# An order among the uses of gathered rows on VectorE, in the expert layer of a two-block model

## The chip, the cores and the metric

The kernel runs on one core of a Trainium2 chip. The metric is device time in microseconds, the median of three runs. The engines are named by what they do: TensorE (PE: matmuls, and PEld: loads of the stationary operand), VectorE (DVE), ScalarE (ACT), GpSimd (POOL) and SyncE (SP), which issues most transfers.

## What is computed

One sequence of 512 tokens plus 16 meta tokens, model width 1024, goes through two blocks. The first mixes tokens (an mLSTM and an attention with a forget gate) and ends in a layer of 16384 experts of one neuron each, of which every token uses 128. The second is a feed-forward layer, a hybrid mixer and a second feed-forward layer. Only the expert layer matters here. Cut to that:

```
def _peer(x, w_query, sub_keys, u_emb, v_emb):      # x: 512 tokens x 1024
    qh = (xb @ w_query).reshape(tb, 8, 2, 128)
    scores = einsum('thpc,hpnc->thpn', qh, keys32)   # 8 heads, 2 halves, 128 keys
    val, idx = lax.top_k(scores, 16)
    ...
    top_s, pos = lax.top_k(cand, 16)
    ids = ...                                        # 128 expert numbers a token
    gate = softmax(top_s)
    act = gelu(einsum('ted,td->te', u_emb[ids], xb))
    return einsum('te,ted->td', gate * act, v_emb[ids])
```

`u_emb` and `v_emb` are 16384 x 1024 float32.

## The kernel before

The expert layer is the method `peer` (L610). It treats the 512 tokens in two ways at once.

The first 384 tokens are computed densely, over all experts, on TensorE. The 16384 experts are 128 blocks of 128. For a block, 24 matmuls give the hidden activations (tile `hp`, a product of the split tokens `xh`, `xl` with a block of u), ScalarE applies the gelu, VectorE multiplies with the gates (`weigh`, L983, the product at L989), ScalarE and VectorE split the result into a high part `eh` and a low part `el` (L245, L250), and 18 matmuls add the block's share of the output into the PSUM tiles `o` (`apply`, L995). Every weight tile is split likewise by `unit` (L144): SyncE loads it into `wr` (L149), ScalarE rounds it to `wh` (L151), and VectorE or GpSimd makes the rest `wl` (L152).

The last 128 tokens are done by rows. Each has 128 experts, so there are 128 slots. For slot n, GpSimd gathers one row of u for each of the 128 tokens by an indirect transfer (tile `row`, 128 x 1024 float32, L643), and VectorE multiplies it with the tokens and sums over the width into a column of `hd3` (L659, a custom instruction and a read of its accumulator). After 128 slots `hd3` holds all activations; ScalarE applies the gelu and VectorE the gates (L661, L662). Then 128 rows of v are gathered in the same way, and each is multiplied by its column of `hd3` and added onto `xtok` (L664 for the first, L666 for the others). The rows share six buffers (`AHEAD + 2`). `own` (L638) issues gather n, and the use of row n - 4; both are placed behind a given VectorE instruction (`behind`, L649), which is how the gathers are paced. 40 gathers are issued while the gates of the dense part are made; the other 216 are spread over the loop of the second half, each behind an L989 product (variable `ws[-1][2]`):

```
                    while len(got) < EARLY + (256 - EARLY) * max(0, spent - REST) // (total - REST):
                        own(ws[-1][2])
```

That loop goes over the 128 blocks in an order that mixes 64 blocks whose activations were made earlier and parked in DRAM (tile `hg`) with 64 that are made now (tile `hd`), so one pass of a pair is one `hd`, one `hg`, 24 + 36 matmuls, and three or four gathers and uses.

The Python code doesn't fix the order in which an engine takes its instructions. A scheduler orders each engine's instructions by their dependencies and its own estimate of times; on the chip an engine then takes them strictly in that order, and one that waits holds all behind it. Uses of v rows depend on one another through `xtok`. Uses of u rows do not: each writes its own column of `hd3`.

Of the kernel before, what the change touches and what calls it, by code (L numbers as in the profile page):

```python
# [94 lines left out]
class Kern:  # L95
# [514 lines left out]
    def peer(self, y):  # L610
        nc, tc, a = self.nc, self.tc, self.a
# [9 lines left out]
        with ExitStack() as ctx:  # L621
# [11 lines left out]
            hd3 = Z.tile([128, 128], F32, name="hd3")  # L633
            rows = {n: a[n].rearrange("a b d -> (a b) d") for n in ("u", "v")}
            got = []
            done = [0]

            def own(after):  # L638

                n = len(got)  # L640
                e, sl = ("u", "v")[n // 128], n % 128
                got.append(Z.tile([128, D], F32, name="row", bufs=AHEAD + 2))
                ld = gp.indirect_dma_start(out=got[n], out_offset=None, in_=rows[e],  # L643
                                           in_offset=bass.IndirectOffsetOnAxis(ap=ids[:, sl:sl + 1], axis=0))
                behind(ld, after)
                if n >= AHEAD:
                    use(after)

            def behind(x, after):  # L649
                tc.add_manual_dep(x.ins, after.ins.name, mybir.DependencyInfo(  # L650
                    mybir.DependencyClass.Sync, mybir.DependencyReason.DATA), reason="pace the gathers")

            def use(after):
                n = done[0]
                done[0] += 1
                e, sl = ("u", "v")[n // 128], n % 128
                row = got[n]
                if e == "u":
                    x = v.tensor_tensor_reduce(row, row, xtok, 1.0, 0.0, OP.mult, OP.add, hd3[:, sl:sl + 1])  # L659
                    if sl == 127:  # L660
                        s.activation(hd3, hd3, AF.Gelu)  # L661
                        v.tensor_tensor(hd3, hd3, gate3, op=OP.mult)  # L662
                elif sl == 0:
                    x = v.tensor_scalar(xtok, row, hd3[:, 0:1], None, op0=OP.mult)  # L664
                else:
                    x = v.scalar_tensor_tensor(xtok, row, hd3[:, sl:sl + 1], xtok, op0=OP.mult, op1=OP.add)  # L666
                behind(x, after)

            with ExitStack() as c1:
                pool1 = lambda n, b=1, **k: c1.enter_context(tc.tile_pool(name=n, bufs=b, reuse_waits="tile", **k))  # L670
# [285 lines left out]
            with ExitStack() as c2:  # L956
# [69 lines left out]
                while done[0] < 256:  # L1026
                    use(ws[-1][2])
# [894 lines left out]
```

## Time and profile before

| | |
|---|---|
| Median of 3 runs | 3293.35 us (3289.94 to 3294.42) |
| The profiled execution: its own time | 3301.91 us |
| its span on the core | 3300.1 us |
| TensorE matmul busy | 3172.1 us, 96% of the span |
| VectorE busy | 1862.5 us, 56% |
| ScalarE busy | 1183.1 us, 36% |
| GpSimd busy | 1064.4 us, 32% |
| Mean granted clock of TensorE | 0.962 |
| First and last use of a u row | 680.7 and 1356.4 us from the span's start |
| First and last use of a v row | 1359.5 and 1788.8 us |

Times within the span are microseconds from its start. A busy share is an average over stages with different limits, so a change to one stage is read in that stage's stretch of the span: the busy time and the granted clock (1.00 is 2.4 GHz, 0.5 is 1.2 GHz) in windows, the waits there, and the order in time of single instructions. In a row of waits, "A <- B" means that A was idle until B ended.

### The profile page before, as it was taken

How to read it: one execution, taken by the hardware profiler on the slowest of the kernel's cores; microseconds unless marked ns; L12 is line 12 of the kernel's file. 1: busy time of each engine (PE TensorE's matmuls, PEld its weight loads, DVE VectorE, ACT ScalarE, POOL GpSimd, SP SyncE). 2: the span in 40 equal slices, each digit the busy share in tenths (PEclk: the TensorE clock that was granted, in tenths of full speed). 3: DMA queues.
4: the chain of work that ended last, by engine and by line, in shares of the span. 5: the costliest groups of instructions: out<-in, count | busy, mean ns of one | idle time of the engine just before them, and what ended most of it. 6: DMA issues, size and time to landing. Idle time of an engine off the chain costs nothing. (4 is left out here: it accounts for less than half of the span.)

```text
span 3300.1 us, 46734 instructions
## 1 busy us (share of the span) xinstructions
PE 3172.1 (96%) x18396; PEld 2794.9 (85%) x18396; DVE 1862.5 (56%) x3481; ACT 1183.1 (36%) x1915; POOL 1064.4 (32%) x676
## 2 busy tenths in 40 slices
PE   8999999799999898999998999989999999989998
PEld 7776788799998787888887999989888889778887
DVE  4342568987755555777887433266434445564324
ACT  3242433344443232333333322235544422332222
POOL 1000134332246675778886211030211002231101
PEclk8888999899999899999999999989999989989999
DMA  3110233377788877889986332232221143423233
GB/s 115 46 48 26 76 97 100 125 265 282 283 301 303 293 272 273 298 317 322 335 307 203 96 91 87 89 118 73 86 68 62 64 136 112 141 77 95 92 93 101
DMA packets 201476, 525.29 MB, mean 159 GB/s; under 512 B 19044, under 2 KB 82440, under 8 KB 199720
## 3 DMA queue, kind: packets, MB, share of 16 engines
q1 hardware_dynamic: 149544, 341.53, 31.5%
q0 software_dynamic: 40624, 142.96, 12.4%
q10 hardware_dynamic: 11088, 37.82, 2.9%
q8 instruction: 144, 2.36, 0.3%
q14 instruction: 76, 0.62, 0.1%
HBM read 470.85 MB, written 51.38 MB: 158 GB/s over the span
## 5 line engine op out<-in xcount | busy, mean ns | idle before, releaser
L151 ACT ACTIVATE wh<-wr 128x1024 fp32r<-128x1024 f32 (+2 forms) x549 | 560.2, 1030 | 1139.7 <-PE fm L89 352.0
L152 DVE TENSOR_TENSOR wl<-wr,wh 128x1024 fp32r<-128x1024 f32 (+1 forms) x371 | 443.0, 1197 | 252.0 <-ACT wh L151 240.7
L152 POOL TENSOR_TENSOR wl<-wr,wh 128x1024 fp32r<-128x1024 f32 (+1 forms) x178 | 438.9, 2480 | 225.1 <-ACT wh L151 224.0
L89 PE MATMUL hp<-xh,wh 128*128 128x384 f32 (+1 forms) x1080 | 377.7, 350 | 0.0
L89 PE MATMUL hp<-xh,wl 128*128 128x384 f32 (+1 forms) x1080 | 373.0, 345 | 4.4 <-DVE wl L152 3.2
L89 PE MATMUL hp<-xl,wh 128*128 128x384 f32 (+1 forms) x1080 | 376.1, 348 | 0.0
L643 POOL DMA_INDIRECT row<-in_u_dram,ids x128 | 196.8, 1538 | 327.0 <-DVE oh L935 213.9
L89 PE MATMUL fm<-xl,wh 128*128 128x264 f32 (+2 forms) x1080 | 280.0, 322 | 0.0
L89 PE MATMUL fm<-xh,wh 128*128 128x264 f32 (+2 forms) x1080 | 277.3, 320 | 1.2 <-DVE u L1173 1.0
L89 PE MATMUL fm<-xh,wl 128*128 128x264 f32 (+2 forms) x1080 | 275.6, 318 | 0.0
L89 PE MATMUL o<-wl,eh 128*128 128x512 f32 x768 | 243.0, 398 | 22.3 <-DVE wl L152 21.9
L659 DVE CUSTOM_DVE_ANT_0 row<-row,xtok 128x1024 f32<-128x1024 f32 x128 | 168.1, 1319 | 164.6 <-DMA row<-in_u_dram,ids 162.8
L89 PE MATMUL mm<-xh,wh 128*128 128x264 f32 (+1 forms) x864 | 245.7, 342 | 14.1 <-ACT wh L151 10.6
L89 PE MATMUL o<-wh,eh 128*128 128x512 f32 x768 | 240.8, 395 | 9.0 <-ACT wh L151 9.0
L89 PE MATMUL mm<-xl,wh 128*128 128x264 f32 (+1 forms) x864 | 245.4, 341 | 1.1 <-DVE xl L252 1.1
L89 PE MATMUL o<-wh,el 128*128 128x512 f32 x768 | 240.5, 395 | 0.0
L89 PE MATMUL mm<-xh,wl 128*128 128x264 f32 (+1 forms) x864 | 239.7, 334 | 0.0
L89 PEld LDWEIGHTS hp<-xh,wl 128*128 128x128 f32 x1080 | 204.7, 190 | 11.9 <-DVE wl L152 3.5
L89 PEld LDWEIGHTS hp<-xh,wh 128*128 128x128 f32 x1080 | 204.5, 189 | 8.3
L89 PEld LDWEIGHTS hp<-xl,wh 128*128 128x128 f32 x1080 | 204.1, 189 | 7.6
L643 POOL DMA_INDIRECT row<-in_v_dram,ids x128 | 182.0, 1422 | 64.3 <-DVE hd L989 33.8
L666 DVE SCALAR_TENSOR_TENSOR xtok<-row,hd,xtok 128x1024 f32<-128x1024 f32 x127 | 196.7, 1548 | 4.5 <-DMA row<-in_v_dram,ids 2.6
(587 smaller groups left out, 6237.4 us busy)
## 6 DMA issues: line engine op xcount, KB each, us to landing
wr<-in_uT_dram SPq DMA_DIRECT2D x128, 512.0 KB, 5.3
wr<-in_v_dram SPq DMA_DIRECT2D x128, 512.0 KB, 6.4
wr<-in_w2in_dram SPq DMA_DIRECT2D x56, 512.0 KB, 3.6
gd<-G ACTq DMA_DIRECT2D x12, 2048.0 KB, 10.1
gi<-gd SPq DMA_DIRECT2D x32, 768.0 KB, 5.5
wr<-in_w2a_i_dram SPq DMA_DIRECT2D x44, 512.0 KB, 3.5
wr<-in_w2b_i_dram SPq DMA_DIRECT2D x44, 512.0 KB, 3.5
hd<-gl ACTq DMA_DIRECT2D x64, 192.0 KB, 4.0
```

What stands on the lines that cost most here:

```text
L89: return self._run(self.tc.nc.tensor.matmul(*a, **k))
L151: for x in (nc.scalar.activation(wh[:, :n], raw[:, :n], AF.Copy), e.tensor_tensor(wl[:, :n], raw[:, :n], wh[:, :n].bitcast(F32), op=OP.sub ...
L152: e.tensor_tensor(wl[:, :n], raw[:, :n], wh[:, :n].bitcast(F32), op=OP.subtract)):
L643: ld = gp.indirect_dma_start(out=got[n], out_offset=None, in_=rows[e], in_offset=bass.IndirectOffsetOnAxis(ap=ids[:, sl:sl + 1], axis=0))
L659: x = v.tensor_tensor_reduce(row, row, xtok, 1.0, 0.0, OP.mult, OP.add, hd3[:, sl:sl + 1])
L666: x = v.scalar_tensor_tensor(xtok, row, hd3[:, sl:sl + 1], xtok, op0=OP.mult, op1=OP.add)
```

## The change

After each use of a gathered row an edge is added from the use issued before it. It is an edge of order alone (NoSync): both stand on VectorE, so no semaphore is waited for; the scheduler may just not place a use ahead of an earlier one.

```
-            done = [0]
+            done, used = [0], []
...
                 behind(x, after)
+                if used:
+                    tc.add_manual_dep(x.ins, used[0], mybir.DependencyInfo(
+                        mybir.DependencyClass.NoSync, mybir.DependencyReason.DATA), reason="in turn")
+                used[:] = [x.ins.name]
```

The instructions of TensorE, ScalarE and GpSimd stand in the same order as before. On VectorE the order differs from the 39th use of a u row to the end of u. In the rows below, `row_8540`, `row_8568`, `row_8932`, `row_8935`, `row_8967`, `row_9032` are the rows of gathers 38 to 43 (counted from 0); a use waits for the semaphore DMASW with the gather's number modulo 8; `wl_...` is the low part of a block of v, `hd_...` the product with the gates of L989 (L993 in the changed kernel, which is four lines longer), `el_...` the low part for TensorE.

VectorE before, around the product hd_8970:

```order
L152 TENSOR_TENSOR wl_9045<-wr_9043,wh_9044 128x1024 [waits DMAHW6_49,Activation_49]
L659 ISA row_8935,hd3_2929<-row_8935,xtok_2926 128x1024 [waits DMASW1_49]
L659 ISA hd3_2929 128x1
L659 ISA row_8967,hd3_2929<-row_8967,xtok_2926 128x1024 [waits DMASW2_49]
L659 ISA hd3_2929 128x1
L989 TENSOR_TENSOR hd_8970<-hd_8970,gi_8806 128x384 [waits Activation_49]
L659 ISA row_8568,hd3_2929<-row_8568,xtok_2926 128x1024 [waits DMASW7_49,DVE_49]
L659 ISA hd3_2929 128x1
L250 TENSOR_TENSOR el_9005<-hd_8970,eh_9004 128x384 [waits Activation_49]
L659 ISA row_8932,hd3_2929<-row_8932,xtok_2926 128x1024 [waits DMASW0_49]
```

Uses 41 and 42 stand ahead of hd_8970, and uses 39 and 40 behind it. The next stretch repeats it: behind the split wl_9148 comes the use of row_9067 (gather 45), then the next product hd_9073, then uses 43 and 44.

VectorE in the changed kernel, the same place:

```order
L152 TENSOR_TENSOR wl_9045<-wr_9043,wh_9044 128x1024 [waits DMAHW6_49,Activation_49]
L993 TENSOR_TENSOR hd_8970<-hd_8970,gi_8806 128x384 [waits Activation_49]
L659 ISA row_8568,hd3_2929<-row_8568,xtok_2926 128x1024 [waits DMASW7_49,DVE_49]
L659 ISA hd3_2929 128x1
L250 TENSOR_TENSOR el_9005<-hd_8970,eh_9004 128x384 [waits Activation_49]
L659 ISA row_8932,hd3_2929<-row_8932,xtok_2926 128x1024 [waits DMASW0_49]
L659 ISA hd3_2929 128x1
L250 TENSOR_TENSOR el_9040<-hg_8839,eh_9039 128x384 [waits PE_49,Activation_49]
L659 ISA row_8935,hd3_2929<-row_8935,xtok_2926 128x1024 [waits DMASW1_49]
L659 ISA hd3_2929 128x1
L659 ISA row_8967,hd3_2929<-row_8967,xtok_2926 128x1024 [waits DMASW2_49]
```

The product hd_8970 now follows the split wl_9045 at once, and uses 39, 40, 41 and 42 come behind it, in turn.

GpSimd, where nothing moves; the gathers of two batches, with the splits between them:

```order
L643 DMA row_8932<-in_u_dram,ids_2927 128x1024 [waits DMASW0_49,DVE_49]
L643 DMA row_8935<-in_u_dram,ids_2927 128x1024 [waits DMASW1_49]
L643 DMA row_8967<-in_u_dram,ids_2927 128x1024 [waits DMASW2_49]
L152 TENSOR_TENSOR wl_9076<-wr_9074,wh_9075 128x1024 [waits DMAHW0_49,Activation_49]
L152 TENSOR_TENSOR wl_9113<-wr_9111,wh_9112 128x1024 [waits DMAHW2_49,PE_49,Activation_49]
L643 DMA row_9032<-in_u_dram,ids_2927 128x1024 [waits DMASW3_49,DVE_49]
L643 DMA row_9035<-in_u_dram,ids_2927 128x1024 [waits DMASW4_49]
L643 DMA row_9067<-in_u_dram,ids_2927 128x1024 [waits DMASW5_49]
L643 DMA row_9070<-in_u_dram,ids_2927 128x1024 [waits DMASW6_49]
```

Each batch waits for VectorE (the DVE semaphore at its head), for a product of L989, and stays behind the two splits ahead of it.

On SyncE one load of a block of v (L149) changes places with two loads of the parked residual stream h (L128, 128 x 512 float32 each); before, it stood behind four of the eight such loads, now behind six.

## Rows read from the trace of the kernel before

**Rows 1.** The page: span, and busy time of each engine (share of the span, instructions).
```profile
span 3300.1 us, 46734 instructions
...
PE 3172.1 (96%) x18396; PEld 2794.9 (85%) x18396; DVE 1862.5 (56%) x3481; ACT 1183.1 (36%) x1915; POOL 1064.4 (32%) x676
```

**Rows 2.** Windows: length; PE, PEld, DVE, ACT, POOL busy (instructions); PEclk, DMA share, GB/s.
```profile
1000.00:1360.00 360.00, 329.98 (x1509) 281.95 (x1508) 195.70 (x300) 105.57 (x149) 242.55 (x139) 0.95 0.78 279
1360.00:1760.00 400.00, 397.85 (x1921) 351.11 (x1920) 317.56 (x274) 144.57 (x196) 330.77 (x183) 1.00 0.90 319
1360.00:1440.00 80.00, 80.00 (x390) 70.91 (x389) 67.88 (x55) 29.21 (x41) 67.75 (x38) 1.00 0.92 333
```

**Rows 3.** Waits, 1000 to 1360 us: who waited for whom; total, times, longest.
```profile
ACT eh L245 <- DVE hd L989: 186.1, 24, 13.5
DVE row L659 <- DMA row<-in_u_dram,ids: 155.9, 26, 9.5
...
PE o L89 <- DVE wl L152: 19.7, 8, 8.3
...
PE o L89 <- ACT wh L151: 9.0, 5, 3.1
```

**Rows 4.** VectorE in order of time: start, length, what [idle before it <- what ended it].
```profile
996.41 0.55 DVE L989 TENSOR_TENSOR hd<-hd,gi 128x384 f32<-128x384 f32 x1
...
1000.24 1.22 DVE L152 TENSOR_TENSOR wl<-wr,wh 128x1024 fp32r<-128x1024 f32 x1
1008.14 1.22 DVE L659 CUSTOM_DVE_ANT_0 row<-row,xtok 128x1024 f32<-128x1024 f32 x1 [6.69 <-DMA row<-in_u_dram,ids]
...
1009.29 0.55 DVE L989 TENSOR_TENSOR hd<-hd,gi 128x384 f32<-128x384 f32 x1
```

**Rows 5.** GpSimd over the same stretch: one batch of gathers, then two splits.
```profile
997.24 1.82 POOL L643 DMA_INDIRECT row<-in_u_dram,ids  x1 [4.46 <-DVE hd L989]
...
1000.96 1.31 POOL L643 DMA_INDIRECT row<-in_u_dram,ids  x1 [0.30 <-issue]
1002.57 0.94 POOL L643 DMA_INDIRECT row<-in_u_dram,ids  x1 [0.30 <-issue]
1003.51 4.75 POOL L152 TENSOR_TENSOR wl<-wr,wh 128x1024 fp32r<-128x1024 f32 x2
```

**Rows 6.** Windows: one stall of TensorE and the clock behind it.
```profile
1088.00:1094.00 6.00, 5.95 (x15) 4.67 (x16) 0.54 (x1) 1.44 (x2) 5.62 (x3) 0.53 1.01 404
1094.00:1100.00 6.00, 6.00 (x33) 5.71 (x32) 5.66 (x10) 4.13 (x6) 3.91 (x3) 1.00 0.73 247
```

**Rows 7.** Waits, 1360 to 1760 us (uses of v rows, already in turn).
```profile
ACT wh L151 <- DMA wr<-in_v_dram: 83.8, 38, 7.8
...
PE o L89 <- DVE wl L152: 2.2, 3, 1.2
```

**Rows 8.** Tile row, 1000 to 1360 us: uses (min/median/max ns), and gathers from issue to landing.
```profile
L659 DVE CUSTOM_DVE_ANT_0 row<-row,xtok x85: 1214/1225/3407, 1008.1 to 1356.4; 128x1024 f32<-128x1024 f32 x85
...
DMA to landing us min/median/max: 4.8/7.0/10.3
```

**Rows 9.** Groups by line, 1000 to 1360 us: count | busy, mean ns | idle before.
```profile
L659 DVE CUSTOM_DVE_ANT_0 row<-row,xtok 128x1024 f32<-128x1024 f32 x85 | 115.5, 1368 | 156.7 <-DMA row<-in_u_dram,ids 155.9
...
L989 DVE TENSOR_TENSOR hd<-hd,gi 128x384 f32<-128x384 f32 x24 | 15.1, 630 | 1.8 <-ACT hd L980 1.8
```

**Rows 10.** Groups by line on VectorE, 1360 to 1760 us.
```profile
L666 DVE SCALAR_TENSOR_TENSOR xtok<-row,hd,xtok 128x1024 f32<-128x1024 f32 x115 | 174.0, 1513 | 1.3
L989 DVE TENSOR_TENSOR hd<-hd,gi 128x384 f32<-128x384 f32 x32 | 62.5, 1954 | 49.2 <-ACT hd L980 49.1
```

**Rows 11.** Windows: the 20 us in which SyncE loads the parked h.
```profile
980.00:1000.00 20.00, 20.00 (x99) 17.74 (x98) 12.87 (x19) 7.40 (x11) 13.93 (x8) 1.00 1.02 368
```

**Rows 12.** VectorE: a use that started beside a GpSimd split.
```profile
1047.91 2.99 DVE L659 CUSTOM_DVE_ANT_0 row<-row,xtok 128x1024 f32<-128x1024 f32 x1 [3.70 <-DMA row<-in_u_dram,ids]
```

**Rows 13.** GpSimd: that split.
```profile
1045.04 4.77 POOL L152 TENSOR_TENSOR wl<-wr,wh 128x1024 fp32r<-128x1024 f32 x2
```

## The prediction

> **What bounds the kernel now.** I read the page first: TensorE is busy 96% of the span [rows 1], so nothing in this kernel is worth time unless TensorE stands still or runs at its lower clock. Which stretch does so, and why, the windows tell. The change touches uses of gathered rows (L659 for u, L664 and L666 for v), so I cut the second half of the expert layer at the place where u ends and v begins, near 1360 us. Over 1000 to 1360 us TensorE is busy 329.98 of 360 us, at a mean granted clock of 0.95; over 1360 to 1760 us it is busy 397.85 of 400 us at 1.00 [rows 2]. Both stretches run the same loop, with the same gathers, weights and matmuls in the same mix; only what is done with a gathered row differs. So the u stretch loses time that the v stretch doesn't, and that is the time at stake.
>
> The waits name the loss. VectorE waits 155.9 us, in 26 pieces of up to 9.5 us, for a gathered u row; ScalarE waits 186.1 us for the product hd (L989) that stands behind these uses; and TensorE waits 19.7 us for wl and 9.0 us for wh [rows 3]. In the v stretch there is no such row among VectorE's waits, and TensorE waits 2.2 us for wl [rows 7].
>
> The timeline shows one piece. VectorE makes hd at 996.41, which releases a batch of gathers; GpSimd issues the first at 997.24, the third at 1000.96, the fourth at 1002.57 [rows 4, 5]. VectorE meanwhile ends its split wl (L152, begun at 1000.24) and then stands for 6.69 us until 1008.14, and only then makes the next hd at 1009.29 [rows 4]. What it waits for is told by the order: the use after the split wl_9148 is that of row_9067, semaphore DMASW5, which is the third gather of that very batch (on GpSimd row_9032, 9035, 9067, 9070). The uses of the first two stand behind hd_9073. So before the change VectorE runs into rows that have been issued only just now, and a gather takes 7.0 us at the median, 10.3 at most, from issue to landing [rows 8]: 1000.96 + 7.0 is 1007.96, against 1008.14 seen. Since hd is queued behind this use, the next batch, the next eh and el, and at last TensorE are late too.
>
> TensorE pays twice: after a gap it ran at 0.53 of its clock from 1088 to 1094 us, in which 15 matmuls ran; in the next 6 us, at 1.00, there were 33 [rows 6].
>
> **The change, part by part.** It adds an edge of order without a semaphore between each use and the one ahead. Nothing is added or taken away in work: the printed orders of TensorE, ScalarE and GpSimd are unchanged, and VectorE has the same instructions in another sequence. That it does nothing is therefore excluded.
>
> *Uses of u rows in the second half.* They now go 38, 39, 40, 41, 42 in the order of the gathers, so a use meets a row of the batch before. Is that early enough? If this stretch takes 314.2 us (below), its 24 products hd [rows 9] come 314.2/24 = 13.1 us apart. The fourth gather of the batch above is issued at 1002.57 and lands at 1009.6 at the median, 1012.9 at worst. Its use comes fourth behind the next hd, at no earlier than 996.41 + 13.1 + 0.55 + 3 x 1.37 = 1014.2 us. So there are 4.6 us to spare at the median, 1.3 at worst; the wait of 155.9 us goes, and with it hd's delay.
>
> *What that is worth on TensorE.* Not 155.9 us, because TensorE's own work covers most of it. I take the rate of the v stretch: 1921 matmuls in 400 us are 4.8025 per us [rows 2]. The 1509 matmuls of the u stretch at that rate need 1509/4.8025 = 314.2 us in place of 360: **45.8 us less**. A second way: TensorE's idle time, 360 - 329.98 = 30.0 us, and the clock, 0.05 x 360 = 18.0 us, make 48.0; less the idle time that the v stretch keeps, 2.15 x 314/400 = 1.7, that leaves 46.3. The bound above is the beginning of the v stretch, which is never idle: 390/80 = 4.875 per us, 309.5 us, 50.5 us less. The bound below is that nothing is given back, or some is lost (the rivals).
>
> *Uses of v rows.* They add onto xtok, so they were in turn already; their order is unchanged. 0 us. The same holds for the first 36 uses of u, ahead of the stretch.
>
> *SyncE.* Two loads of the parked h go ahead of one weight of v instead of behind it, near 982 to 990 us. 2 x 0.26 MB at 368 GB/s are 1.4 us by which that weight may come later. In that window TensorE is never idle, at clock 1.00 [rows 11], so I take 0; bounds 0 and 1.4 us.
>
> *What is late next.* In the v stretch ScalarE waits 83.8 us for v weights and VectorE 49.1 us for ScalarE's hd [rows 7, 10], and TensorE still loses 2.15 us. I expect that picture in the u stretch.
>
> *Two engines that read SBUF at once.* A use begun at 1047.91 took 2.99 us where the median is 1.225 [rows 8]; a pair of GpSimd splits ran from 1045.04 to 1049.81 [rows 12, 13], and the use ended 1.0 us after them. The Trainium skill (SBUF — State Buffer, section "Who interferes with whom") says that a VectorE instruction with two inputs in SBUF and a GpSimd instruction that reads SBUF contend, and that whichever starts first keeps the shared ports for its whole length. By that rule, and the trace agrees with it here, a VectorE that no longer waits for rows will meet more of these splits. The rows give the size: in the v stretch, where VectorE is that dense, a use has a mean of 1.513 us and hd 1.954 us, against 1.368 and 0.630 in the u stretch [rows 9, 10]. That adds 85 x 0.145 + 24 x 1.324 = 44 us to VectorE's 195.7 us [rows 2]: 240 of 314 us, still not the bound. I take 0 us.
>
> The sum is -45.8 us. The profiled execution, 3301.91 us, would become 3256.1; it lay 8.56 us above the median of the runs shown, 3293.35, and from that median the sum gives 3247.6. I say **3248 us**. Profiling may have made the waits a little longer than they are in a plain run; the range covers that.
>
> **Rivals.**
> *Late gathers.* With hd every 13.1 us, GpSimd has one pair of splits (4.75 us) and a batch (997.24 to 1003.5, 6.3 us) in each: 11 of 13.1 us [rows 5]. A slip of over 1.3 us makes a late gather late for its use. If half of the 155.9 us came back, TensorE's loss would halve as well: 22.9 us gained, about 3270. Against it: the v stretch runs this batch at 4.80 matmuls per us without a wait for rows.
> *The feed.* 279 GB/s are moved in the u stretch [rows 2]. If weights and gathers could not come faster there, ScalarE would wait for weights in place of VectorE for rows, and the time stays at 3293. Against it: the v stretch moves 319, and its first 80 us 333; the u stretch would need 279 x 360/314 = 320.
> *VectorE held by GpSimd (slower).* Mechanism as above: uses held for the whole of a split. If every use came to the length of the longest, 3.407 us [rows 8], VectorE would need 195.7 + 85 x (3.407 - 1.368) = 369 us, more than the 360 that the stretch takes now: +9 us, about 3302. The gain begins to shrink at a mean use of 1.368 + (314.2 - 195.7)/85 = 2.76 us, and turns at 1.368 + (360 - 195.7)/85 = 3.30. Against it: 1.513 in the v stretch [rows 10].
>
> **How the numbers follow.** A measurement of this kernel can tell about 0.2%, 6.6 us, from no change. Chances: the forecast 0.78 (its own range 3239 to 3257, from the 50.5 us bound and 3 us of spread between runs down to four fifths of the gain), late gathers 0.12, the feed 0.05, VectorE held 0.04, something else 0.01. The range runs from 3239 to 3273, through the case of late gathers; the last two cases lie outside. Faster: 0.78 + 0.12 + 0.01 = 0.91; same 0.05; slower 0.04.
>
> **What would show it.** Right: no row "DVE row L659 <- DMA row" of more than some 10 us in all; the u stretch, 1509 matmuls, in 310 to 318 us at a clock of 0.99 or 1.00, and TensorE's wait for wl there at a few us; the v stretch unchanged in length, some 45 us earlier; DMA near 320 GB/s. Late gathers: that L659 row at 50 to 100 us. The feed: it is gone, but ScalarE's waits for weights have grown by as much. VectorE held: L659 with a mean over 2.7 us. The prediction is wrong if the row of 155.9 us goes and TensorE's idle time in the stretch stays near 30 us, for then another wait set the pace.

## The result, and the profile after

The changed kernel takes 3254.02 us (four runs, 3249.46 to 3254.39), the one before 3293.89 us (four runs, 3289.94 to 3295.03): a ratio of 0.9881, 95% interval 0.9867 to 0.9895. The gain is 39.9 us, where 45.8 were worked out. It is faster, the mechanism is the one forecast, and the sum came out about 6 us too large.

The page of the changed kernel, against [rows 1]:

```profile
span 3252.0 us, 46763 instructions
...
PE 3152.9 (97%) x18396; PEld 2789.3 (86%) x18396; DVE 1905.1 (59%) x3481; ACT 1186.1 (36%) x1915; POOL 1078.4 (33%) x676
```

The two spans differ by 48.1 us, more than the medians do, because the profiled execution of before lay 8.0 us above the median of its four runs and this one does not (its own time is 3253.81 us). In the spans, 9.1 us lie ahead of the first u use, which comes at 671.6 us in place of 680.7 and which no edge of the change can move. From there to the last u use it is 635.7 us in place of 675.7: 40.0 us, all of the gain. The v uses take 428.8 us, from 1310.3 to 1739.1, in place of 429.3.

So the u stretch to compare with 1000 to 1360 us [rows 2] is now 1000 to 1314 us, and the v stretch 1314 to 1714 us. The windows of the changed kernel (columns as in [rows 2]):

```profile
1000.00:1314.00 314.00, 308.97 (x1479) 271.74 (x1478) 230.85 (x294) 106.82 (x146) 250.29 (x135) 0.99 0.89 313
1314.00:1714.00 400.00, 398.07 (x1925) 351.90 (x1923) 315.53 (x274) 143.54 (x195) 329.44 (x181) 1.00 0.90 318
1220.00:1240.00 20.00, 18.33 (x86) 15.55 (x86) 19.90 (x24) 9.71 (x14) 17.92 (x10) 1.00 0.82 271
1260.00:1280.00 20.00, 17.68 (x75) 14.72 (x73) 11.13 (x17) 5.75 (x8) 12.81 (x8) 0.91 0.79 279
1280.00:1300.00 20.00, 18.96 (x88) 16.10 (x89) 10.21 (x13) 5.72 (x8) 15.80 (x9) 1.00 0.78 264
```

TensorE now idles 5.0 us in the u stretch where it idled 30.0, and its clock is 0.99 where it was 0.95. All 5.0 us lie in the last three windows (1.67 + 2.32 + 1.04). The v stretch has the rate that it had before: 1925 matmuls in 400 us, against 1921.

The waits of the changed kernel, 1000 to 1314 us, against [rows 3]:

```profile
ACT eh L245 <- DVE hd L993: 89.9, 23, 10.1
ACT wh L151 <- DMA wr<-in_v_dram: 61.5, 20, 9.4
DVE hd L993 <- ACT hd L984: 44.5, 12, 8.8
...
DVE hg L993 <- DMA hg<-hd: 20.8, 4, 6.1
...
ACT wh L151 <- DMA wr<-in_uT_dram: 16.5, 7, 11.3
DVE hg L993 <- issue: 16.2, 3, 6.2
...
PE o L89 <- DVE wl L152: 3.2, 2, 1.7
...
PE hp L89 <- POOL wl L152: 1.8, 1, 1.8
...
DVE row L659 <- DMA row<-in_u_dram,ids: 0.9, 1, 0.9
```

VectorE's wait for gathered rows fell from 155.9 us to 0.9. ScalarE's for hd fell from 186.1 to 89.9, TensorE's for wl from 19.7 to 3.2. What VectorE waits for now stands ahead of the uses: ScalarE's hd (44.5 us) and, at the products of hg, the parked activations (20.8 us) and something that the profile doesn't show (16.2 us, "issue").

The timeline of VectorE shows the place of the uses:

```profile
1002.02 1.22 DVE L152 TENSOR_TENSOR wl<-wr,wh 128x1024 fp32r<-128x1024 f32 x1
1008.30 1.96 DVE L993 TENSOR_TENSOR hg<-hg,gi 128x384 f32<-128x384 f32 x4 [5.06 <-issue]
1010.18 0.55 DVE L993 TENSOR_TENSOR hd<-hd,gi 128x384 f32<-128x384 f32 x1
1010.77 1.23 DVE L659 CUSTOM_DVE_ANT_0 row<-row,xtok 128x1024 f32<-128x1024 f32 x1
...
1012.39 1.22 DVE L659 CUSTOM_DVE_ANT_0 row<-row,xtok 128x1024 f32<-128x1024 f32 x1
...
1014.00 1.22 DVE L659 CUSTOM_DVE_ANT_0 row<-row,xtok 128x1024 f32<-128x1024 f32 x1
...
1015.15 1.22 DVE L659 CUSTOM_DVE_ANT_0 row<-row,xtok 128x1024 f32<-128x1024 f32 x1
```

Between the split wl and hd no use is left, and four uses follow hd with no wait. In [rows 4] a use stood between the two and waited 6.69 us.

Lines of VectorE, 1000 to 1314 us (count | busy, mean ns | idle before), against [rows 9]:

```profile
L659 DVE CUSTOM_DVE_ANT_0 row<-row,xtok 128x1024 f32<-128x1024 f32 x84 | 121.9, 1461 | 1.7 <-DMA row<-in_u_dram,ids 0.9
...
L993 DVE TENSOR_TENSOR hd<-hd,gi 128x384 f32<-128x384 f32 x23 | 43.8, 1905 | 44.5 <-ACT hd L984 44.5
```

Both have become longer, to 1461 from 1368 ns and to 1905 from 630 ns, nearly the means of the v stretch [rows 10]. VectorE is busy 230.85 of 314 us; 240 were forecast. Laying the timelines of VectorE and GpSimd over each other tells where the longer products come from: 13 of the 23 products hd now overlap a GpSimd split by over 0.3 us, at a mean of 2.94 us, and the other ten have 0.56. Before, it was one of 24.

### The profile page after: what moved, and what is told of

The parts are those of the page before. It is cut to its first block, busy times and chain, and to the rows that moved or that the text cites. A ratio compares the mean times of both kernels' runs of the same rounds, so it can differ in the third digit from the quotient of the medians.

```text
span 3252.0 us, 46763 instructions
## 1 busy us (share of the span) xinstructions
PE 3152.9 (97%) x18396; PEld 2789.3 (86%) x18396; DVE 1905.1 (59%) x3481; ACT 1186.1 (36%) x1915; POOL 1078.4 (33%) x676
## 5 line engine op out<-in xcount | busy, mean ns | idle before, releaser
L643 POOL DMA_INDIRECT row<-in_u_dram,ids x128 | 208.0, 1625 | 263.9 <-DVE oh L939 207.2
L1179 POOL TENSOR_TENSOR u<-u,R 128x528 f32<-128x528 f32 (+1 forms) x44 | 74.7, 1700 | 378.8 <-ACT u L1178 378.8
```

The costliest lines, as they stand in the source:

```text
L1179: nc.gpsimd.tensor_tensor(u, u, R, op=OP.mult)
```

## The experiments

Four sets of runs were made, and the kernel before took 3293.89, 3290.95, 3288.25 and 3293.24 us in them. So versions are compared by their ratio to the before of their own set. The theory was that the gain is the place of the uses on VectorE: behind hd, at rows that have landed. The rivals were that it is the edge itself, the number of rows in hand, or the transfers.

### The edges on the first part of the stretch only

```
-                if used:
+                if used and n < 82:
```

> The edges of order are kept for the first 82 uses of a row and left out for the others, so u rows 38 to 81 are used in turn and from 82 on VectorE meets each cycle a row of the batch that was issued in the same cycle. Theory (what costs time is a use that stands ahead of the product hd and meets a row of its own batch, about one to two each cycle): the gain of 40 us comes in proportion to the cycles put in turn, about half, so some 3274 us; VectorE's wait for u rows in the second half 70 to 90 us, all of it in the later part of u. Rival (the gain comes from something that happens once, such as the start of the loop or the loads of h): 3254 us if it lies early, 3294 us if late.

Measured: 3273.02 us, 0.9948 (0.9935 to 0.9961). Its windows, then its row wait ahead of 1150 us and behind it:

```profile
1000.00:1160.00 160.00, 157.94 (x762) 138.99 (x761) 108.35 (x143) 51.09 (x70) 120.38 (x65) 1.00 0.85 300
1160.00:1340.00 180.00, 161.76 (x735) 137.85 (x734) 104.80 (x152) 55.48 (x79) 123.76 (x71) 0.94 0.80 282
```

```profile
DVE row L659 <- DMA row<-in_u_dram,ids: 7.5, 2, 6.6
```

```profile
DVE row L659 <- DMA row<-in_u_dram,ids: 77.9, 14, 9.4
```

The 83rd use, the first that no edge holds, is also the first to wait as before; ahead of it the row waits are 0.9 us in all:

```profile
1141.16 1.23 DVE L659 CUSTOM_DVE_ANT_0 row<-row,xtok 128x1024 f32<-128x1024 f32 x1 [6.57 <-DMA row<-in_u_dram,ids]
```

Up to 1160 us, where the edges hold all but the last 19 us, TensorE runs 762/160 = 4.76 matmuls per us; behind that it runs 735/180 = 4.08. The wait came back to 85.4 of 155.9 us, 55%, and the gain left is 0.0052 of 0.0119, 44%. Gain and wait go together, in place and in size.

### In turn, but close behind the gathers

All uses stay in turn. In the second half, use n is issued with gather n + 1 (or n + 2) in place of n + 4.

```
-                if n >= AHEAD:
+                while done[0] <= n - (1 if late2 else AHEAD):
                     use(after)
...
                 E = pool2("px", 1)
+                late2.append(E)
```

> The changed kernel, all uses in turn, but in the second half of the expert layer a row is used one slot behind its gather instead of four, so three uses a cycle meet rows of the batch of the same cycle; the v rows too. Theory (it is the distance from gather to use that counts, not the turn itself): the wait for u rows is back, 140 us or more, and the v stretch, which lost nothing before, waits likewise; 40 us lost in u and 45 to 60 us in v, so 3335 to 3355 us. Rival (uses in turn are enough, whatever the distance): 3254 us.

> The changed kernel, all uses in turn, with a use two slots behind its gather in the second half instead of four (one slot gave 3379.6 us, four give 3254.0 us). The last use of a cycle then meets the second gather of the same cycle's batch instead of the third; gathers of a batch are issued 1.6 us apart. Theory (a cycle is longer by the time from the release of the batch to the landing of the latest row used in it, less what TensorE's work covers): the loss is smaller than at one slot by about 1.6 us in each of some 60 cycles, that is 95 of 125 us or less, so 3280 to 3330 us. Rival (only the turn, or only whether any row of the own batch is met): 3254 or about 3380 us.

Measured: distance one 3379.57 us, 1.0264 (1.024 to 1.0288); distance two 3326.92 us, 1.0108 (1.0093 to 1.0124). With the same edges the kernel is slower than before, so being in turn does not gain by itself; a use must also lie far enough behind its gather. Distance two lies within its forecast, and its rival (no difference between one slot and two) is out. VectorE's waits for rows, at distance one (970 to 1350 us) and at distance two (970 to 1780 us):

```profile
DVE row L660 <- DMA row<-in_u_dram,ids: 113.7, 41, 6.2
```

```profile
DVE xtok L667 <- DMA row<-in_v_dram,ids: 86.2, 42, 5.0
DVE row L660 <- DMA row<-in_u_dram,ids: 67.1, 33, 6.4
```

Two parts of the forecast for distance one missed. The wait for u rows is 113.7 us, where 140 or more were expected. And the loss was larger than expected, with the excess in the v stretch: 516.3 us from its first use to its last, where the changed kernel takes 428.8. Its windows, u then v:

```profile
970.00:1350.00 380.00, 346.08 (x1600) 292.93 (x1598) 264.76 (x319) 110.29 (x157) 257.04 (x143) 0.99 0.79 282
1350.00:1780.00 430.00, 387.89 (x1744) 326.73 (x1744) 308.33 (x251) 125.16 (x178) 294.49 (x164) 0.97 0.74 269
```

and the uses of v rows among its lines of VectorE, 1350 to 1780 us:

```profile
L667 DVE SCALAR_TENSOR_TENSOR xtok<-row,hd,xtok 128x1024 f32<-128x1024 f32 x103 | 222.6, 2161 | 121.7 <-DMA row<-in_v_dram,ids 119.5
```

All of VectorE's idle time, 121.7 of these 430 us beside 308.3 of work, lies at this one line: it waits for no other engine, so its own work and these rows set the pace. A use costs 430/103 = 4.17 us of its time; in the changed kernel it was 400/115 = 3.48 in the v stretch, a fifth of that idle. 128 uses at 0.70 us more are 89 us, and 87.5 were lost. Part of it is not the wait: the mean use is 2161 ns long, against 1513 [rows 10].

### More rows in hand, no edges

The kernel before, without edges, with ten row buffers in the second half in place of six (four of them the tile `rowe`), and use n issued with gather n + 8.

```
-                got.append(Z.tile([128, D], F32, name="row", bufs=AHEAD + 2))
+                got.append(late2[0].tile([128, D], F32, name="rowe", bufs=4) if late2 and n % 10 > 5 else
+                           Z.tile([128, D], F32, name="row", bufs=AHEAD + 2))
...
-                if n >= AHEAD:
+                while done[0] <= n - (8 if late2 else AHEAD):
```

> The kernel before, without edges of order, but with ten row buffers instead of six in the second half and a use eight slots behind its gather instead of four. Its VectorE order still has in nearly each cycle one or two uses of rows of the same cycle's batch ahead of the product hd. Theory: no gain, 3285 to 3298 us, and a wait for u rows of 120 us or more. Rival (six buffers are too few, so that a use out of turn keeps a buffer from the next gather; or the distance written in the program is what counts): 3254 to 3260 us, the wait nearly gone.

Measured: 3298.72 us, 1.0023 (1.0011 to 1.0035). Waits, 980 to 1400 us:

```profile
DVE row L661 <- DMA row<-in_u_dram,ids: 93.0, 17, 10.2
DVE rowe L661 <- DMA rowe<-in_u_dram,ids: 46.0, 9, 9.2
```

With more rows in flight, 139.0 us of waiting stay. The order still put a use or more of a fresh batch ahead of hd. More buffers don't help while the order has VectorE take such a row first.

### No gathers at all in the u stretch

```
+                if EARLY <= n < 128:
+                    got.append(got[n - 2])
+                    use(after)
+                    return
...
-                    x = v.tensor_tensor_reduce(row, row, xtok, 1.0, 0.0, OP.mult, OP.add, hd3[:, sl:sl + 1])
+                    x = v.tensor_tensor_reduce(row, xtok if n >= EARLY else row, xtok, 1.0, 0.0, OP.mult, OP.add, hd3[:, sl:sl + 1])
```

> The changed kernel without the 88 gathers of u rows in the second half (the transfers are left out; the uses of these slots take the tokens themselves in place of a row). It measures what is left to gain in the u stretch, where TensorE was idle some 5 us of 314 and 1.8 us went to the lower clock. Theory (what is left comes from weights that arrive late because gathers share the transfer queues): the stretch loses its idle time and the kernel takes 3246 to 3250 us. Rival (the weights are late for want of weight buffers, whatever else is moved): 3254 us. A time well below 3244 us would say that gathers cost something else that I have not seen.

Measured: 3248.07 us, 0.9867 (0.9848 to 0.9887), an interval that overlaps the changed kernel's. Its u stretch:

```profile
980.00:1300.00 320.00, 317.10 (x1528) 279.44 (x1527) 265.24 (x309) 113.18 (x155) 137.02 (x56) 1.00 0.55 181
```

At 181 GB/s in place of 313 TensorE still idles 2.9 of 320 us. So all that the transfers and issues of these 88 gathers still cost in the changed kernel is about 0.0014 of the time, some 5 us, and the runs don't tell that from nothing.

### The residue: weight buffers and the tail

Two edits on the changed kernel, alone and together: four weight buffers in the second half in place of three,

```
-        raw = self.wp.tile([128, 1024], F32, name="wr", bufs=3)
+        raw = (self.raws.tile([128, 1024], F32, name="wr", bufs=4) if self.raws else
+               self.wp.tile([128, 1024], F32, name="wr", bufs=3))
```

and the last gathers six steps of the loop earlier.

```
-                    while len(got) < EARLY + (256 - EARLY) * max(0, spent - REST) // (total - REST):
+                    while len(got) < min(256, EARLY + (256 - EARLY) * max(0, spent - REST) // (total - REST - 6)):
```

> The changed kernel with four buffers for weights as they come from DRAM, instead of three, in the second half of the expert layer. Without the 88 gathers 6 us more were gained, and ScalarE's waits for weights of v fell. Theory A (what is left of TensorE's idle time there comes from weights that could have been asked for earlier): 3247 to 3252 us. Theory B (the transfer queues are busy 0.9 in that stretch and more weights asked for at once only wait longer): 3253 to 3256 us.

> The changed kernel, with the gathers of the second half spread so that the last one falls six steps (of 184) before the loop ends, instead of at its end. In the changed kernel the last six uses of v rows run from 1726 to 1742 us, behind the last products, and TensorE waits 5.4 us for them and then runs at 0.55 of its clock for some 10 us. Theory: 6 to 10 us of that go, 3244 to 3249 us. Rival (denser gathers bring the waits for rows or weights back in the loop): 3254 us or more.

> Both of the above edits. If they are independent the gains add: 3238 to 3249 us, the sum of the two within 3 us. If the earlier gathers and the additional weight buffer compete for the same transfers, no better than the better of the two.

Measured: 0.9891 (0.9872 to 0.9909), 0.9880 (0.9865 to 0.9895) and 0.9881 (0.9866 to 0.9896). None is told from the changed kernel. The reason to try the buffers was ScalarE's timeline in the changed kernel, in the windows where TensorE idles, and what TensorE then waits for:

```profile
1269.84 1.06 ACT L151 ACTIVATE wh<-wr 128x1024 fp32r<-128x1024 f32 x1 [11.27 <-DMA wr<-in_uT_dram]
1270.80 0.47 ACT L984 ACTIVATE hd<-hp 128x384 f32<-128x384 f32 x1
```

```profile
1273.38 0.44 PE L89 MATMUL hp<-xh,wl 128*128 128x384 f32 x1 [1.81 <-POOL wl L152]
```

With four buffers the windows are these, and TensorE has one wait in the stretch:

```profile
1000.00:1314.00 314.00, 306.89 (x1470) 270.74 (x1469) 237.44 (x293) 107.59 (x147) 251.34 (x135) 0.98 0.88 313
1220.00:1300.00 80.00, 80.00 (x388) 70.72 (x387) 66.16 (x79) 29.62 (x41) 68.49 (x37) 1.00 0.93 324
```

```profile
PE o L89 <- DVE wl L154: 7.1, 1, 7.1
```

and ScalarE's waits for weights, which were 61.5 and 16.5 us, are

```profile
ACT wh L153 <- DMA wr<-in_v_dram: 1.8, 2, 0.9
ACT wh L153 <- DMA wr<-in_uT_dram: 1.5, 1, 1.5
```

The late weights at 1220 to 1300 us are gone, and the idle time isn't: it stands in one piece elsewhere. So these late weights are where the residue was seen, not what must be removed to be rid of it. The earlier gathers gave something in the tail, where TensorE idles 2.7 us from 1720 to 1750 us against 7.8 in the changed kernel, and lost as much in the loop:

```profile
960.00:1300.00 340.00, 329.64 (x1573) 289.20 (x1572) 255.95 (x314) 114.31 (x155) 263.95 (x143) 0.99 0.89 315
```

that is 10.4 us idle in 340, against 5.0 in the changed kernel. What sets the residue stays open.

### The place without the edge

The kernel before, no edges. A use in the second half is placed behind the last product of hd, in place of the last product of either kind.

```
-            got = []
+            got, paced = [], []
...
-                    use(after)
+                    use(paced[0] if paced else after)
...
                         spent += order[n] >= NA
+                        if order[n] >= NA:
+                            paced[:] = [ws[-1][2]]
```

> The kernel before, without any of the added edges; only the pace of the uses is changed: in the second half a use is placed behind the last product of hd instead of behind the last instruction that VectorE was given, which may be a product of hg that runs up to four blocks early. If the gain of the change is the place of the uses among the products of hd, and the chain of edges was only one way to set it, this version gains as much: a ratio of 0.986 to 0.990 (about 3,253 us against 3,293), and VectorE waits at the row transposes for arriving rows for under 15 us between 980 and 1,400 us, where it waited 155.9 us. If the edge from one use to the next does something else (it holds uses together, or keeps them behind the gathers), this version stays at 0.995 to 1.002 with over 100 us of that wait.

A second version places the gathers behind the last hd too; and the changed kernel ran again beside them.

> As the version with the pace of the uses alone, and the gathers of the second half are placed behind the last product of hd too. The theory of the place of the uses: 0.986 to 0.990, no more than with the uses alone, since a gather that is issued earlier than it need be costs nothing. If the weights that arrive late at 1,220 to 1,300 us in the changed kernel are late because the gathers come too early and bunched, a gather paced by the products of hd should take 2 to 5 us off: 0.9850 to 0.9865.

> The changed kernel as it is, on the same chip as the two paced versions, so that they can be set against it: a ratio of 0.987 to 0.990, and both paced versions within 0.1% of it if the place of the uses is all that counts.

(The "row transposes" of the first text are the uses of rows, L659.) Measured: uses alone 3256.23 us, 0.9885 (0.9866 to 0.9905); gathers as well 3261.54 us, 0.9907 (0.989 to 0.9925); the changed kernel 3260.62 us, 0.9894 (0.9875 to 0.9913). Waits of the first, VectorE, 980 to 1400 us:

```profile
DVE hd L989 <- ACT hd L980: 58.6, 19, 9.1
DVE hg L989 <- DMA hg<-hd: 28.3, 5, 6.6
DVE hg L989 <- issue: 17.6, 3, 6.3
DVE row L659 <- DMA row<-in_u_dram,ids: 1.5, 1, 1.5
```

Without a single edge the row wait is 1.5 us and the gain is that of the change. This shows the cause. Each use had been placed behind the last product that was issued. That is in part a product of hg, which needs nothing of the present block: hg products run four at a time (the row of 1008.30 above), some blocks early, and so hold no use back. A use paced by one was free to go ahead of hd; a use paced by an hd product was not. Counted through the loop of the source, 34 of the 92 uses of u rows placed there are paced by a product of hg. Uses 41, 42 and 45, which stood ahead of hd before the change, are among them; uses 39, 40, 43 and 44, which stood behind it, are not. The chain of edges ties the first kind to the second. Pacing the gathers by hd as well brings nothing (it is 0.13% above the changed kernel, where the text gave 0.1%, and the intervals overlap), so the gathers were not too early.

## Why the prediction was right, and where it was off

*What bounds the kernel.* Right. The waiting uses ahead of hd were the loss, and taking them away gave it back. The v stretch was the right measure for the u stretch: 1479/314 = 4.71 matmuls per us came out, 4.80 were taken. At that rate the 1509 matmuls of before would take 320.4 us, a little outside the 310 to 318 that were named as a sign of being right. Nothing shows that profiling lengthened the waits: from the first u use to the last the two profiles differ by 40.0 us, the medians by 39.9.

*How the wait became time.* The text said that TensorE's own work covers most of the 155.9 us. The two profiles allow a sharper reading. Before, VectorE was busy 195.7 of 360 us [rows 2] and idle 156.7 at the uses and 1.8 at hd [rows 9], and at hg:

```profile
L989 DVE TENSOR_TENSOR hg<-hg,gi 128x384 f32<-128x384 f32 x28 | 13.7, 552 | 5.7 <-DMA hg<-hd 5.7
```

Together 359.9 of 360 us. Work and idle time of any engine fill a stretch; what tells is whom it waits for. Nearly all of VectorE's idle time was for gathered rows, and the gathers in turn wait for VectorE's product:

```profile
POOL row L643 <- DVE hd L989: 81.6, 22, 8.1
```

So the circle runs from hd to the gather, to its landing, to the use and to the next hd, and TensorE is not in it. A VectorE that shows as 54% busy was the pace of the loop, its waits being in series with its work. The version with half of the edges says the same of its unordered part: 104.8 us of work, 69.5 of row waits and 5.2 of hg are 179.5 of 180. When the row wait goes, VectorE needs about 231 us, TensorE 309, and TensorE sets the pace; the gain ends there, not at 155.9. In these two versions a stretch lasts as long as VectorE's work and row waits together, or as TensorE's work, whichever is more.

*The mis-sized term.* It is the idle time that the stretch keeps: "less the idle time that the v stretch keeps, 2.15 x 314/400 = 1.7", with a clock of 1.00. Measured are 5.0 us of idle time, 3.3 more than that, and a clock of 0.99 (rounded; it fell only in the window from 1260 to 1280 us, by 0.09 x 20 = 1.8 us): 5.1 us. By the rate, 1479 matmuls at 4.8025 are 308.0 us, and they took 314: 6.0 us. The gain was forecast 5.9 us too large. The u stretch is not quite the v stretch, and I took the cleanest rate that the trace had as the likeliest.

*Landing in time.* Right: 4.6 us to spare at the median were worked out, and the row wait is 0.9 us in one piece.

*v uses, SyncE.* Right: 428.8 against 429.3 us for the v uses. Counted from the first u use they begin 40 us earlier, where some 45 were forecast.

*Late gathers* fell, by the row wait. The runs at distances one and two show that this rival's mechanism is real: it decides some gathers closer.

*The feed* did not hold the stretch. DMA moved 313 GB/s, near the 320 that the stretch was said to need. ScalarE's waits for weights are 78.0 us (61.5 + 16.5); in the version with four weight buffers they are 3.3 us, and its time isn't told from the changed kernel's.

*VectorE held by GpSimd* fell as a bound: the mean use is 1461 ns, where the gain was to shrink from 2.76 us. That a VectorE which no longer waits would meet more GpSimd splits held for the products hd (13 of 23 against one of 24) and not for the uses (6 of 83 against 9 of 85). But single uses are longer than the longest before (3.407 us [rows 8]). In the changed kernel, VectorE and then GpSimd:

```profile
1237.77 6.17 DVE L659 CUSTOM_DVE_ANT_0 row<-row,xtok 128x1024 f32<-128x1024 f32 x1
```

```profile
1236.09 1.98 POOL L643 DMA_INDIRECT row<-in_u_dram,ids  x1 [0.30 <-issue]
1238.10 4.75 POOL L152 TENSOR_TENSOR wl<-wr,wh 128x1024 fp32r<-128x1024 f32 x2
```

The use ended at 1243.94, 1.1 us after the pair of splits. The Trainium skill (SBUF — State Buffer, section "Who interferes with whom") has it that a VectorE instruction with two inputs in SBUF and a GpSimd instruction that reads SBUF contend; the length of this use agrees. It also says that whoever starts first keeps the ports. The use began 0.33 us ahead of the pair and was yet the one held, but GpSimd was then still issuing a gather (until 1238.07), so these rows don't decide who came first.

## What to carry to other kernels

Add an engine's busy time and its waits for one kind of data over a stretch. If they fill the stretch, and the transfers of that data are themselves released by the same engine, the circle through that engine sets the pace, however low its busy share. The gain of removing the wait ends where the next engine's own work begins. On an engine that works in order, a consumer of late data belongs behind the instruction that feeds the other engines, and far enough behind its load. If it is held there by an edge, tie it to an instruction that really runs at that time: one that the scheduler may take blocks ahead holds nothing.

## What the runs showed that was not expected

The same number of microseconds of row waits cost very different times. By ratio to the changed kernel and with 3293 us: the kernel before lost 39 us with 155.9 us of waits, the version at distance two lost 75 us with 153.3 (67.1 at u, 86.2 at v). One reason is the room that VectorE has: 81.5 of 314 us in the u stretch of the changed kernel (44.5 + 20.8 + 16.2), and less in its busier v stretch, 315.53 of 400 us busy. That can't be all: the 67.1 us at u would have fitted into the room there, and yet the u uses took 658.7 us from first to last, against 635.7. The uses had also become longer. At distance two, u from 980 to 1330 us and v from 1340 to 1750:

```profile
L660 DVE CUSTOM_DVE_ANT_0 row<-row,xtok 128x1024 f32<-128x1024 f32 x89 | 180.3, 2031 | 64.9 <-DMA row<-in_u_dram,ids 64.0
```

```profile
L667 DVE SCALAR_TENSOR_TENSOR xtok<-row,hd,xtok 128x1024 f32<-128x1024 f32 x105 | 225.6, 2148 | 82.9 <-DMA row<-in_v_dram,ids 81.7
```

In the changed kernel a u use has a mean of 1461 ns. The timelines of VectorE and GpSimd show which uses are the long ones. At distance two 24 of these 89 uses of u overlap a GpSimd split by over 0.3 us, at a mean of 4.22 us, and the other 65 have 1.22; at distance one it is 31 of 92 (3.45, the others 1.24); in the changed kernel 6 of 83 (4.26, the others 1.25). So a use close behind its gather meets these splits more often. How much of the loss comes from that and how much from the wait was not tried apart.
